# Attention tiles of two heads by 64 queries, with three transposed blocks per two chunks

## The chip, the cores and the metric

The kernel runs on one core of one Trainium2 chip. Its engines are named as in the profile: PE (matmuls; PEld is its weight load), DVE, ACT and POOL (elementwise work), and SP, which issues nearly all transfers. The metric is the device time of one execution in microseconds.

## The reference

One inference step of a two-layer encoder on 1024 prompt frames and 32 sample frames, model width 1024. The first layer is a recurrent mixer, the second a sliding-window attention with 16 query heads and 2 shared key/value heads of width 64. Both are followed by a gated feed-forward network. The change touches the attention only:

```python
CHUNK = 64; WINDOW = 128          # a chunk of 64 queries sees its own and the two chunks before: 192 keys
alibi = -slopes.reshape(N_KV_HEADS, GROUP, 1, 1) * jnp.abs(dist).astype(F32)
bias = jnp.where((key_pos >= 0)[:, None, None, None, :], alibi[None], -jnp.inf)[None]
s = jnp.einsum('bcqhgd,bckhd->bchgqk', q, k).astype(F32) * (HEAD_DIM ** -0.5) + bias
mx = jnp.maximum(jnp.max(s, -1, keepdims=True), sk)      # sk: a learned sink score per head
p = jnp.exp(s - mx)
p = p / (jnp.sum(p, -1, keepdims=True) + jnp.exp(sk - mx))
return jnp.einsum('bchgqk,bckhd->bcqhgd', p.astype(v.dtype), v)
```

The 32 sample queries see 128 cached keys and the 32 keys of the sample.

## The kernel before

**Number format.** Each fp32 operand of a large product is split into a high part (`hi`, cast by ACT) and a remainder (`lo`, subtracted on DVE or POOL). A product is then three matmuls (L402 to L404: hi by hi, hi by lo, lo by hi). In the attention, a query tile carries hi in one half of its partitions and lo in the other, so a product with K's high and low parts is two matmuls.

**Order of the work.** All engines run their instructions in the order in which the program emits them. The order is written out by the program itself: `gemm` emits the dense products and, after every three matmuls, calls `wv.tick(us)` with an estimate of their time. Tasks (Python generators) each count down a pause and then emit their next piece. So attention work is woven between dense matmuls, and a pause is a measure of how much dense work goes in between. `wv.drain` emits a task's pieces at once, with nothing between.

**Tokens.** They come in three groups (`GRP`: 384, 384, 288) for the projections, and in nine blocks of 128 (`CH`; the ninth is the 32 sample tokens). A head pair `j` (0 to 7) is 128 columns of the query projection. `q_group(j, g)` (L1651) projects one pair for one group: 24 matmuls, then ACT writes `qh` (L1657), DVE `ql` (L1658), and `place` sends them with four transfers (L1664, L1665) into a tile `Q` of which there are four. `qh` and `ql` have two buffers each.

**Attention.** `attention` walks over 72 items: head pair `j` by block `b`. Five stages make an item, run in a software pipeline in which `turn` and `values` each lag by one item or more:

- `scores` (L1763, L1764): per head, a product of 128 queries with the 256 keys of this block and the one before (two matmuls of 256 columns, for K's high and low parts); then DVE adds the bias, takes the row minimum (the scores are negated) and writes `s` (L1769). Half of the 256 keys' edge chunks lie outside of a query's window, and the bias holds a large constant there. Block 0 has 128 keys, the sample block 160.
- `soft` (L1781, L1785, L1787): ACT's exponential with its row sum, the reciprocal on DVE, and the scaling on POOL, one per head.
- `turn` (L1807 to L1811): transposes on PE of the 128 by 128 blocks of `s` (two heads by two key blocks, four; two for block 0) into one PSUM tile `T`, which has one buffer; ACT casts it to `hi`, DVE subtracts to `lo`.
- `values` (L1822, L1823): V's 128 keys by 128 columns (high and low part side by side) with `hi` and with `lo`, for both heads at once (256 columns), into the PSUM tile `O` (two buffers).
- `place` (L1831, L1833): ACT copies the lower half of `O`, DVE adds the halves into `act`.

The projections of the pairs to come are emitted in the order `QG`, each once enough items are scored (`ast["scored"]`). Bias tiles `bt`, `sb` are loaded per visit of a head pair, 12 of each (L1689, L1690), with the sinks copied into their last column by POOL (L1697, L1698). `v_turn` (L1736) transposes V through the buffers of `O`, with the casts at L1678 and L1679. One weight half has a place of its own outside of the rotating weight slots (`W.home`, tile `oh`). The weight split is ACT's cast at L237 and POOL's or DVE's subtraction at L239; the load of the next raw weights (`wr`, L163) waits for a raw buffer on SP's queue. After the attention `mixer_out` starts the output projection; `before(0)` (L1900) first drains the attention up to a given item.

## Time and profile before

| | |
|---|---|
| time, median of 3 runs | 2210.78 us (2210.55 to 2211.94) |
| profiled execution: span | 2212.2 us |
| PE busy / DVE / ACT / POOL | 98% / 66% / 46% / 45% |
| granted PE clock, mean | 0.997 |
| matmuls in the whole program | 17086 |
| of these: scores / transposes of s / values | 288 / 272 / 272 |

The span is the time from the first to the last instruction of the one execution that was profiled; there is no other time of that execution, and it stands 1.4 us above the median of the runs. Times are counted from the start of the span. A row of a timeline gives start, duration, engine, line, operation, the tile written and those read, and in brackets the idle time before it and what ended that. "128*128" after a matmul is rows by weight columns of the array. SPq marks the issue of a transfer, not the transfer.

### The profile page before, as it was taken

Reading aid. Unit: us, or ns where it says so; the run is one execution under the profiler, and the core shown is the slowest. Engines: PE = TensorE matmul, PEld = TensorE weight load, DVE = VectorE, ACT = ScalarE, POOL = GpSimd, SP = SyncE. Lnnn points to the kernel's source line nnn. Section 1 sums busy time; section 2 is a strip of 40 time slices with the busy share of each in tenths; the row PEclk is TensorE's granted clock in tenths of the full one; section 3 lists DMA queues with packets and bytes.
Section 4 is the critical chain, followed back from the end, with each engine's and each line's share of the span. In section 5 each row is a group of like instructions: output and inputs, shape, how many; then the busy total and the mean of one; then the engine's idle time right before and its main releaser. Section 6 shows DMA issues by size and latency. Waiting matters only on the chain.

```text
span 2212.2 us, 44257 instructions
## 1 busy us (share of the span) xinstructions
PE 2175.5 (98%) x17086; PEld 2149.4 (97%) x17086; DVE 1455.2 (66%) x2848; ACT 1007.9 (46%) x2259; POOL 989.8 (45%) x982
## 2 busy tenths in 40 slices
PE   9999999999999999999998999999999999999997
PEld 9999999999999999999998999899999999999997
DVE  4465677787656665566667778888666656466657
ACT  4443455464444444321245778756444444432125
POOL 2544210004655555444525776600665555554441
PEclk9999999999999999999999999999999999999999
DMA  5221213212443343797516433511344434397712
GB/s 170 78 62 57 58 40 87 89 39 86 148 156 145 139 147 135 254 329 231 175 57 174 108 100 97 156 63 39 112 161 156 146 127 156 132 344 256 247 56 79
DMA packets 174499, 298.10 MB, mean 135 GB/s; under 512 B 18064, under 2 KB 130760, under 8 KB 174288
## 3 DMA queue, kind: packets, MB, share of 16 engines
q1 hardware_dynamic: 169936, 290.94, 40.0%
q10 hardware_dynamic: 4352, 4.33, 0.6%
q8 instruction: 135, 2.21, 0.4%
q14 instruction: 76, 0.62, 0.1%
HBM read 201.80 MB, written 82.94 MB: 129 GB/s over the span
## 4 chain that ended last, share of the span: by engine, by line
PE 85%; DVE 6%; DMA 3%; ACT 3%; issue 1%; POOL 1%; SPq 0%; ACTq 0%; POOLq 0%; DVEq 0%
PE d L402 10%; PE d L404 10%; PE d L403 10%; PE A L402 9%; PE A L404 9%; PE A L403 9%; PE B L402 7%; PE B L403 7%; PE B L404 7%; DMA sx<-hs_t 1%; PE T L1807 1%; ACT act L505 1%; DMA hs_x<-z 1%; POOL s L1787 1%; PE T L955 1%
## 5 line engine op out<-in xcount | busy, mean ns | idle before, releaser
L239 POOL TENSOR_TENSOR wl_s<-wr,wh_s 128x512 fp32r<-128x512 f32 x224 | 304.1, 1367 | 237.4 <-ACT wh_s L237 168.9
L402 PE MATMUL d<-sx,wh 128*128 128x264 f32 (+2 forms) x1068 | 341.8, 320 | 2.1 <-ACT wh L237 1.8
L239 POOL TENSOR_TENSOR wl_a<-wr,wh_a 128x512 fp32r<-128x512 f32 x112 | 153.5, 1373 | 409.4 <-ACT wh_a L237 288.2
L404 PE MATMUL d<-sx,wl 128*128 128x264 f32 (+2 forms) x1068 | 325.9, 305 | 2.7 <-POOL wl L239 2.7
L403 PE MATMUL d<-sx,wh 128*128 128x264 f32 (+2 forms) x1068 | 325.3, 305 | 0.4 <-DVE sx L433 0.4
L402 PE MATMUL A<-sx,wh_s 128*128 128x264 f32 x896 | 254.7, 284 | 0.0
L403 PE MATMUL A<-sx,wh_s 128*128 128x264 f32 x896 | 254.4, 284 | 0.0
L404 PE MATMUL A<-sx,wl_s 128*128 128x264 f32 x896 | 254.3, 284 | 0.0
L237 ACT CAST wh_s<-wr 128x512 fp32r<-128x512 f32 x224 | 135.7, 618 | 192.6 <-DVE wr L192 102.7
L402 PEld LDWEIGHTS d<-sx,wh 128*128 128x128 f32 x1068 | 202.3, 189 | 5.5 <-ACT wh L237 2.4
L404 PEld LDWEIGHTS d<-sx,wl 128*128 128x128 f32 x1068 | 201.7, 189 | 3.9 <-POOL wl L239 3.6
L403 PEld LDWEIGHTS d<-sx,wh 128*128 128x128 f32 x1068 | 202.6, 190 | 1.5 <-DVE sx L433 0.7
L402 PE MATMUL d<-sx,ex 128*128 128x264 f32 x624 | 180.7, 290 | 0.1
L403 PE MATMUL d<-sx,ex 128*128 128x264 f32 x624 | 177.3, 284 | 0.0
L404 PE MATMUL d<-sx,ex 128*128 128x264 f32 x624 | 177.1, 284 | 0.0
L404 PEld LDWEIGHTS A<-sx,wl_s 128*128 128x128 f32 x896 | 169.0, 189 | 0.0
L402 PEld LDWEIGHTS A<-sx,wh_s 128*128 128x128 f32 x896 | 168.6, 188 | 0.0
L403 PEld LDWEIGHTS A<-sx,wh_s 128*128 128x128 f32 x896 | 168.6, 188 | 0.0
L1323 POOL TENSOR_TENSOR z<-z 128x528 fp32r<-128x528 f32 x76 | 103.2, 1357 | 126.8 <-ACT z L1322 113.3
L239 POOL TENSOR_TENSOR wl<-wr,wh 128x512 fp32r<-128x512 f32 (+2 forms) x81 | 103.9, 1291 | 94.5 <-ACT wh L237 90.7
L1787 POOL TENSOR_SCALAR s<-s,st 128x256 f32<-128x256 f32 (+1 forms) x144 | 122.8, 865 | 46.6 <-DVE st L1785 29.2
L402 PE MATMUL A<-ex,wh_s 128*128 128x264 f32 x448 | 127.5, 285 | 0.0
(352 smaller groups left out, 7247.4 us busy)
## 6 DMA issues: line engine op xcount, KB each, us to landing
wr<-in_gu SPq DMA_DIRECT2D x92, 512.0 KB
hs_x<-z SPq DMA_DIRECT2D x72, 528.0 KB
hs_t<-z SPq DMA_DIRECT2D x64, 528.0 KB
sx<-hs_x SPq DMA_DIRECT2D x112, 264.0 KB
sx<-hs_t SPq DMA_DIRECT2D x64, 264.0 KB
ex<-hs_t SPq DMA_DIRECT2D x64, 264.0 KB
wr<-in_dn SPq DMA_DIRECT2D x32, 512.0 KB
ex<-hs_x SPq DMA_DIRECT2D x32, 264.0 KB
```

Of the source, the lines that this page charges most:

```text
L237: self.nc.scalar.copy(hi, r)
L239: eng.tensor_sub(lo, r, hi.bitcast(F32))
L402: nc.tensor.matmul(out, ah, bh, start=start and k == 0, stop=False, **kw)
L403: nc.tensor.matmul(out, ah, bl, start=False, stop=False, **kw)
L404: nc.tensor.matmul(out, al, bh, start=False, stop=stop and k == last, **kw)
L505: nc.scalar.activation(z, z, AF.Identity, scale=gk, bias=bk)
L955: nc.tensor.matmul(pc[:, : 2 * (DV + 1)], keys, vt[j][:, c], start=True, stop=True)
L1323: eng.tensor_sub(lo.bitcast(F32R), buf(s), hi)
L1787: nc.gpsimd.tensor_scalar_mul(p[:R, h, lo:256], p[:R, h, lo:256], st[:R, 2, h : h + 1])
L1807: nc.tensor.transpose(pt[:nk, i, h, :R], p[:R, h, c : c + nk], ident[:R, :R])
```

## The change

The attention tile becomes two heads by 64 queries (128 rows) with exactly the 192 keys that these see; an item still covers one head pair and one block, now as two such tiles (chunks `c`) side by side in one score bank, so the two banks alternate between items.

- **Q's layout.** `Q` holds, chunk by chunk, 64 tokens of the first head beside 64 of the second; the transfers write pieces of 64 columns, and a group of 288 tokens needs eight. `qh` and `ql` have one buffer.
- **Scores and softmax.** Per chunk two matmuls of 192 columns. The bias has one table of 64 queries by 192 keys per head, on 128 rows, without a constant for unseen keys; the sink column stands before the first chunk and after the second. The scaling on POOL is one product with a broadcast operand for both chunks.
- **Transposes.** The 384 columns of an item's two chunks are three blocks of 128. The middle one holds the last 64 keys of the first chunk and the first 64 of the second.
- **Values.** Two head pairs (items `2 jp` and `2 jp + 1`) share one product per chunk and part. For the middle block V is taken from a tile `VZ` that is zero for the other chunk's keys; `pad_values` fills it by transfers, once for each key/value head.
- **PSUM.** `T` has two buffers and serves V's transposes as well; `O` has one, of a whole bank. `place` runs once per two items.
- **Order.** Head pairs are visited two by two: `JG` lists these twos (`jp`) by group, six items for each entry, and `QG` their projections. The two projections of an entry are emitted one after the other once all items up to the entry before the last are scored. Bias tables are loaded once per `jp`; the place of its own for one weight half goes. `GAP_A` goes from 0.46 to 0.5, and the pause after `values` is 0 and twice that in turn.

The diff, cut to its core:

```diff
-GAP_A = 0.46
+GAP_A = 0.5
...
-        q = Q[j, g] = new(pb, "Q", [P, 2, 384], F32R, bufs=4)
-        h, l = (new(pb, tag, [P, 384], F32R, bufs=2)[:, :n] for tag in ("qh", "ql"))
+        q = Q[j, g] = new(pb, "Q", [P, 2 * 384], F32R, bufs=4)
+        h, l = (new(pb, tag, [P, 384], F32R)[:, :n] for tag in ("qh", "ql"))
...
-                nc.sync.dma_start(q[own, i, :n].bitcast(F32), h[own].bitcast(F32))
-                nc.sync.dma_start(q[other, i, :n].bitcast(F32), l[own].bitcast(F32))
+                for t, src in ((own, h), (other, l)):
+                    for a, m in ((0, LC * (n // LC)), (LC * (n // LC), n % LC)):
+                        if m:
+                            w = min(m, LC)
+                            d = q[t, 2 * a : 2 * a + 2 * m].rearrange("p (c h w) -> p c h w", h=2, w=w)
+                            r = src[own, a : a + m].rearrange("p (c w) -> p c w", w=w)
+                            nc.sync.dma_start(d[:, :, i].bitcast(F32), r.bitcast(F32))
...
+    B, SB = {}, {}
+
+    def load_bias(jp):
+
+        bt = B[jp] = new(pb, "bt", [P, 2, WK + 2], bufs=3)
+        nc.sync.dma_start(bt[:, :, 1 : WK + 1], A["bias"][:, 2 * jp : 2 * jp + 2, :])
+        for h in range(2):
+            r = slice(64 * h, 64 * h + 64)
+            for c in (0, WK + 1):
+                nc.gpsimd.tensor_copy(bt[r, :, c], nsink[r, 4 * jp + h : 4 * jp + 4 : 2])
+
+    def load_sample_bias(jp):
+
+        sb = SB[jp] = new(pb, "sb", [2 * DEC, 2, P + DEC + 1])
+        nc.sync.dma_start(sb[:, :, 1:], A["sbias"][:, 2 * jp : 2 * jp + 2, :])
+        for h in range(2):
+            r = slice(DEC * h, DEC * h + DEC)
+            nc.gpsimd.tensor_copy(sb[r, :, 0], nsink[r, 4 * jp + h : 4 * jp + 4 : 2])
 
     load_bias(0)
-    load_bias(1, False)
+    load_bias(1)
+    load_bias(2)
+    load_sample_bias(0)
...
+    ENDS = (1, 2 * WK + 2)
+    for t in psS:
+        for c in ENDS:
+            nc.vector.memset(t[:, c : c + 1], 0.0)
 
     pb2 = eb.enter_context(pool("pb2"))
-    W.home[U_QB[1][5], 1] = [new(pb2, "oh", [P, D // 2], F32R, bufs=2)[:] for _ in range(2)]
     psb = eb.enter_context(pool("psb", PSUM))
+    VZ = [pb2.tile([P, 8, 2 * HD], F32R, name=f"VZ{i}") for i in range(2)]
+    for i in range(2):
+        nc.gpsimd.memset(VZ[i][64 * (1 - i) : 64 * (2 - i)].bitcast(F32), 0.0)
+
+    def pad_values(tiles, g2):
+
+        for i in range(2):
+            r = slice(64 * i, 64 * i + 64)
+            v = VR[r, tiles, g2].rearrange("p t a d -> p t (a d)")
+            nc.sync.dma_start(VZ[i][r, tiles].bitcast(F32), v.bitcast(F32))
 
...
-                pt = new(psb, "O", [P, 512], bufs=2)
+                pt = new(psb, "T", [P, 512], bufs=2)
                 nc.tensor.transpose(pt[:L, :P], vT[g][:, off : off + L], ident[:])
                 v_parts(c, pt[:L, :P], L)
+                if c % 3 == 2:
+                    pad_values(slice(c - 2, min(c + 1, 8)), 0)
                 ast["v"] = c + 1
...
+    JG = [(0, 0), (1, 0), (0, 1), (0, 2), (1, 1), (1, 2)]
+    JG += [(2, 0), (2, 1), (2, 2), (3, 0), (3, 1), (3, 2)]
+    QG = [(2 * jp + i, g) for jp, g in JG for i in range(2)]
+
+    def last_item(j, g):
+        return 6 * JG.index((j // 2, g)) + 6
+
...
+        def parts(b):
+
+            if b == 0:
+                return [(0, 130, 64, 0, 1 + P), (1, 258, P, 0, 1 + LC)]
+            if b == 8:
+                return [(0, 2, P + DEC, SEQ, 1)]
+            k0 = (b - 1) * P
+            return [(0, 2, WK, k0, 1), (1, 2 + WK, WK, k0 + LC, 1)]
 
         def scores(j, b):
             _, t0, R, g, off = CH[b]
+            jp = j // 2
+            if (j, b) == (4, 0):
+                load_bias(3)
             s = S[j, b] = {}
+            q, g2, ps = Q[j, g], j // 4, psS[j % 2]
+            bias = SB[jp] if b == 8 else B[jp]
+            p = s["p"] = new(pb2, "s", [P, 2 * WK + 4], bufs=4)
             st = s["st"] = new(pb2, "st", [P, 3, 2], bufs=6)
+            n = DEC if b == 8 else LC
+            rows = 2 * n
+            if b == 0:
+                nc.vector.memset(ps[:, 194:195], 0.0)
+            for c, at, nk, k0, _ in parts(b):
+                lhs = q[:, 2 * (off + n * c) : 2 * (off + n * c) + rows]
+                for i, k in enumerate((KH[g2], KL[g2])):
+                    nc.tensor.matmul(ps[:rows, at : at + nk], lhs, k[:, k0 : k0 + nk], start=i == 0, stop=i == 1)
+            for c, at, nk, _, w in parts(b):
+                first = b != 0 and c == 0
+                cols = slice(at - first, at + nk + (not first))
+                bc = slice(w - first, w + nk + (not first))
                 nc.vector.tensor_tensor_reduce(
+                    p[:rows, cols], ps[:rows, cols], bias[:rows, j % 2, bc], 1.0, 3e38,
+                    op0=ALU.add, op1=ALU.min, accum_out=st[:rows, 0, c : c + 1],
                 )
+            if b == 8 and j % 2 and jp < 3:
+                load_sample_bias(jp + 1)
             ast["scored"] += 1
 
         def soft(j, b):
             s = S[j, b]
             p, st = s["p"], s["st"]
+            rows = 2 * DEC if b == 8 else P
+            for c, at, nk, _, _ in parts(b):
+                first = b != 0 and c == 0
+                cols = slice(at - first, at + nk + (not first))
                 nc.scalar.activation(
+                    p[:rows, cols], p[:rows, cols], AF.Exp, bias=st[:rows, 0, c : c + 1], scale=-1.0,
+                    accum_out=st[:rows, 1, c : c + 1],
                 )
+            n = len(parts(b))
+            nc.vector.reciprocal(st[:rows, 2, :n], st[:rows, 1, :n])
+            if 0 < b < 8:
+                w = p[:, 2 : 2 + 2 * WK].rearrange("p (c k) -> p c k", c=2)
+                nc.gpsimd.tensor_mul(w, w, st[:, 2].unsqueeze(2).broadcast_to([P, 2, WK]))
+            else:
+                for c, at, nk, _, _ in parts(b):
+                    w = p[:rows, at : at + nk]
+                    nc.gpsimd.tensor_scalar_mul(w, w, st[:rows, 2, c : c + 1])
+
+        def blocks(b):
 
             if b == 0:
+                return [(1, 130, 64), (2, 258, P)]
             if b == 8:
+                return [(0, 2, P), (1, 130, DEC)]
+            return [(t, 2 + t * P, P) for t in range(3)]
 
         def turn(j, b):
+            s = S.pop((j, b))
             p = s["p"]
+            rows = 2 * DEC if b == 8 else P
+            if j % 2 == 0:
+                pairs_[j // 2, b] = {
+                    tag: new(pb2, tag, [P, 3, 2, P], F32R, bufs=2) for tag in ("hi", "lo")
+                }
+            s = pairs_[j // 2, b]
+            pt = new(psb, "T", [P, 512], bufs=2).rearrange("p (t r) -> p t r", t=4)
+            for t, at, nk in blocks(b):
+                nc.tensor.transpose(pt[:nk, t, :rows], p[:rows, at : at + nk], ident[:rows, :rows])
+            cuts = [(slice(0, 3), P)] if 0 < b < 8 else [(slice(t, t + 1), nk) for t, _, nk in blocks(b)]
+            hi, lo = (s[x][:, :, j % 2, :] for x in ("hi", "lo"))
+            for t, nk in cuts:
+                nc.scalar.copy(hi[:nk, t, :rows], pt[:nk, t, :rows])
+                nc.vector.tensor_sub(lo[:nk, t, :rows], pt[:nk, t, :rows], hi[:nk, t, :rows].bitcast(F32))
 
         def values(j, b):
 
+            if j % 2 == 0:
+                return
+            s = pairs_[j // 2, b]
             g2 = j // 4
+            po = s["po"] = new(psb, "O", [P, 2, 2, P])
+            full = lambda i: VR[:, i, g2].rearrange("p a d -> p (a d)")
+            if b == 0:
+                sums = [[(1, full(0), 64)], [(2, full(0), P)]]
+            elif b == 8:
+                sums = [[(0, full(9), P), (1, full(8), DEC)]]
+            else:
+                sums = [
+                    [(0, full(b - 1), P), (1, VZ[0][:, b], P)],
+                    [(1, VZ[1][:, b - 1], P), (2, full(b), P)],
+                ]
+            rows = 2 * DEC if b == 8 else P
+            for c, terms in enumerate(sums):
+                out = po[:, c, :, :rows]
+                todo = [(v, s[x][:nk, t, :, :rows], nk) for t, v, nk in terms for x in ("hi", "lo")]
+                for i, (v, x, nk) in enumerate(todo):
+                    nc.tensor.matmul(out, v[:nk], x, start=i == 0, stop=i == len(todo) - 1)
+            if (j, b) == (3, 7):
+                pad_values(slice(0, 8), 1)
 
         def place(j, b):
             _, t0, R, g, off = CH[b]
+            ast["placed"] += 1
+            if j % 2 == 0:
+                return
+            po = pairs_.pop((j // 2, b))["po"]
+            n, nc_ = (DEC, 1) if b == 8 else (LC, 2)
+            t = new(pb2, "t", [HD, 2, 2, P])
+            rows = 2 * n
+            nc.scalar.copy(t[:, :nc_, :, :rows], po[HD:, :nc_, :, :rows])
             for h in range(2):
+                out = ACT[h * HD : (h + 1) * HD, j - 1 : j + 1, t0 : t0 + R].rearrange("p j (c q) -> p c j q", c=nc_)
+                a, b_ = (x[:HD, :nc_, :, n * h : n * h + n] for x in (po, t))
+                nc.vector.tensor_add(out, a, b_)
 
         always = lambda j, b: True
         yield 4.0
         yield from pipeline(
+            [(2 * jp + i, 3 * g + b) for jp, g in JG for b in range(3) for i in range(2)],
             [
+                (scores, lambda j, b: ast["ready"] > QG.index((j, CH[b][3])), 0, (gap,) * 8),
                 (soft, always, 0, 0),
+                (turn, always, 1, (gap,) * 8),
+                (values, lambda j, b: ast["v"] > b, 1, (0.0, 2 * gap) * 4),
                 (place, always, 0, 0),
             ],
             (4, 2, 3, 1, 0),
         )
 
 
...
-        while ast["scored"] < 3 * (i - 3):
+        while ast["scored"] < 6 * (i // 2 - 1):
...
-                    lambda k, g: ast["placed"] >= 3 * QG.index((k, g)) + 3,
+                    lambda k, g: ast["placed"] >= last_item(k, g),
...
-            wv.drain(task, lambda: ast["placed"] >= 3 * QG.index((7, 0)) + 3)
+            wv.drain(task, lambda: ast["placed"] >= last_item(7, 0))
```

Of the attention stages the diff shows the lines after the change; those before it are in the listing above. `...` stands for lines left out, the tables of the bias (`_bias`, now 64 queries by 192 keys, and 32 by 160 for the sample) among them.

108 lines of the change are left out of this document (11 added, 97 removed).

## The prediction

> **What bounds the kernel now.** I read the page first: the engines' sums, then the chain that ended last.
>
> ```profile
> span 2212.2 us, 44257 instructions
> ...
> PE 2175.5 (98%) x17086; PEld 2149.4 (97%) x17086; DVE 1455.2 (66%) x2848; ACT 1007.9 (46%) x2259; POOL 989.8 (45%) x982
> ...
> PE 85%; DVE 6%; DMA 3%; ACT 3%; issue 1%; POOL 1%; SPq 0%; ACTq 0%; POOLq 0%; DVEq 0%
> ```
>
> PE is busy nearly throughout and holds 85% of the chain. So the change is worth what it takes off PE's queue, plus the PE idle time that it removes, less what it adds. The busy time by stretches shows where PE idles around the attention, which runs from about 1197 to 1426 us (columns: length, then PE, PEld, DVE, ACT, POOL busy, granted clock, DMA share, GB/s).
>
> ```profile
> 1200.00:1220.00 20.00, 17.34 (x106) 16.12 (x107) 10.40 (x48) 11.18 (x38) 13.75 (x19) 0.91 0.60 159
> ...
> 1260.00:1280.00 20.00, 20.00 (x152) 19.54 (x151) 15.02 (x60) 15.92 (x50) 16.97 (x24) 1.00 0.48 133
> ...
> 1400.00:1420.00 20.00, 17.06 (x130) 15.89 (x129) 15.98 (x53) 14.96 (x46) 17.68 (x19) 0.93 0.39 119
> ```
>
> In the middle PE is full. It idles at the start and at the end of the attention, and there the granted clock dips too (0.91, 0.93). So I cost three things apart: PE's own work, the idle time inside the stage, and the start.
>
> **PE's work, part by part.** Matmuls overlap, so a duration of 280 ns is not a price; the distance between starts is. PE's timeline gives it (start, duration, operation, shape).
>
> ```profile
> 1206.80 0.28 PE L1763 MATMUL psS<-KH,Q 128*128 128x128 f32 x1
> 1206.91 0.28 PE L1764 MATMUL psS<-KL,Q 128*128 128x128 f32 x1
> ...
> 1210.31 0.38 PE L1807 MATMUL T<-ident,s 128*128 128x128 f32 x2
> ...
> 1251.87 0.28 PE L1763 MATMUL psS<-KH,Q 128*128 128x256 f32 x1
> ...
> 1252.34 0.30 PE L402 MATMUL d<-sx,wh 128*128 128x288 f32 x1
> ...
> 1252.75 0.60 PE L1807 MATMUL T<-ident,s 128*128 128x128 f32 x4
> ...
> 1257.66 0.24 PE L1763 MATMUL psS<-KH,Q 128*32 128x160 f32 x1
> ...
> 1257.95 0.38 PE L402 MATMUL d<-sx,wh 128*128 128x384 f32 x1
> ...
> 1414.79 0.19 PE L1822 MATMUL O<-hi,VR 128*128 128x64 f32 x1
> ...
> 1415.36 0.39 PE L402 MATMUL d<-sx,wh 128*128 128x264 f32 x1
> ```
>
> Transposes: a run of four lasts 0.60 us, a run of two 0.38, so one costs (0.60 - 0.38) / 2 = 0.11 us. An inner item (two heads, 128 queries, b = 1 to 7; 56 of them) goes from four to three: 56 x 0.11 = 6.2 us. The eight items of b = 0 keep two. The eight of b = 8 go from four small ones to two: between 0 and 16 x 0.11 = 1.8 us, I take 0.8.
>
> Scores: four products of 256 columns fill 1251.87 to 1252.34, 0.117 us each. They become four of 192 columns, still with 128 weight columns (two heads by 64 queries). No row has that shape. The nearest with 128 weight columns has 128 columns and takes 0.11 (1206.80 to 1206.91), so fewer columns buy almost nothing: 56 x 4 x 0.007 = 1.6 us. The other end is the product of 160 columns with only 32 weight columns: four in 0.29 us, 0.073 each, scaled to 192 columns 0.088: 56 x 4 x 0.029 = 6.5 us. I take 1.6, because the weight width is what the changed shape shares with the first row. The Trainium skill, page "TensorE: Matmul & The Clock Gate", section "Back-to-back issue gap", gives N/2.4 + 2.5 ns, which is an estimate of 82 ns for 192 columns and would make this term 7.8 us; its section "LDWEIGHTS (loading the stationary operand)" gives columns/1.2, 107 ns for 128 weight columns, and the 110 ns above agree with that one. For b = 8, four products of 0.073 become two (weights 32 to 64 columns): 16 x 0.073 = 1.2 us less. For b = 0 there are four at 0.11 in both: nothing.
>
> Values: one product now takes two head pairs, but one 64-query chunk. Per two inner items that is eight products of 256 columns in both kernels: nothing saved. For b = 8, two runs of 0.57 us (1414.79 to 1415.36) become one of four 128-column products, 0.44 to 0.57: four times 0.57 to 0.70, I take 2.5 us.
>
> Sum: 6.2 + 0.8 + 1.6 + 1.2 + 2.5 = **12.3 us less PE work** (10 to 18).
>
> **Idle time inside the stage.** What PE waits for before a run of transposes, and the work that the change makes lighter (rows grouped by line and shape: busy time, mean ns, idle time before it; then two waits from PE's timeline):
>
> ```profile
> L1807 PE MATMUL T<-ident,s 128*128 128x128 f32 x240 | 38.2, 277 | 6.7 <-DVE lo L1811 4.0 <-POOL s L1787 1.1 <-DVE st L1785 1.0
> L1787 POOL TENSOR_SCALAR s<-s,st 128x256 f32<-128x256 f32 x112 | 102.6, 929 | 40.1 <-DVE st L1785 25.1 <-PE psS L1764 7.0 <-PE T L1807 4.2
> L239 POOL TENSOR_TENSOR ex<-wr,ex 128x384 fp32r<-128x384 f32 x24 | 23.5, 1045 | 0.0
> ...
> 1413.60 0.63 PE L1807 MATMUL T<-ident,s 128*128 128x128 f32 x4 [0.95 <-DVE lo L1811]
> ...
> 1417.45 1.09 PE L1807 MATMUL T<-ident,s 128*128 128x128 f32 x4 [1.45 <-DVE lo L1811]
> ```
>
> The waits for lo exist because T has one buffer: a run can't start until DVE has read the last one. T gets two (O drops to one, which is used once per two items). POOL's two products of 0.93 us per inner item become one over 384 columns; the nearest POOL row of two operands and 384 columns is 1.05 us, so the waits for s shrink as well. ACT and DVE read a quarter fewer score and T columns. The 6.7 us of idle time stand for about ten waits; each also loses the overlap of one transpose (0.277 - 0.11 = 0.17 us), 1.7 us, and the dip of the clock after 1417.45 costs (1 - 0.93) x 20 = 1.4 us: 9.8 us in all. What is late next is the exponentials on ACT. I let the change remove **7 us** (3 to 9.8).
>
> **The start.** The head-pair projections write qh and ql (L1657, L1658), which SP's transfers read into Q. The change makes both tiles single-buffered. The chain of waits already runs through this reuse, with two buffers:
>
> ```profile
> 1195.00 5.22 DMA Q<-qh
> 1200.33 0.49 ACT qh L1657
> 1200.82 0.52 ACT wh L237
> 1201.36 0.56 DVE ql L1658
> ...
> 1202.31 0.48 PE O L1736
> ```
>
> Here the fourth projection's qh (1200.33) waited until the second's transfers were out of the buffer; behind it on ACT stands the cast of V, and PE's third transpose of V waits for that. The timelines of ACT, POOL, SP and PE add what sets the third projection's transfers:
>
> ```profile
> 1198.11 0.49 ACT L1657 ACTIVATE qh<-d 128x384 fp32r<-128x384 f32 x1
> ...
> 1199.19 1.27 POOL L239 TENSOR_TENSOR wl<-wr,wh 128x512 fp32r<-128x512 f32 x1 [0.62 <-ACT wh L237]
> ...
> 1200.48 0.33 SPq L163 DMA_DIRECT2D wr<-in_wqb  x1
> 1200.86 0.46 SPq L1664 DMA_DIRECT2D Q<-qh  x1
> ...
> 1202.01 0.60 SPq L1664 DMA_DIRECT2D Q<-qh  x1
> ...
> 1202.31 0.48 PE L1736 MATMUL O<-ident,act 128*128 128x128 f32 x1 [2.80 <-DVE VR L1679]
> ```
>
> With one buffer the third qh waits for the second's transfers, until 1195.00 + 5.22 = 1200.2 instead of 1198.11: 2.1 us. Behind it ACT's weight cast, POOL's rest (L239), SP's load of wr and so the third's transfers move by as much. The fourth qh then waits for the last qh transfer of the third, issued at 1202.01: landing 2.2 us (nothing else in flight, an estimate) to 5.2 us later gives 1204.2 to 1207.2, plus 2.1. Against 1200.33 that is 6 to 9 us, and the V transposes follow it with nothing else in PE's queue to go first. I take **7.5 us more** (5 to 11; the upper end if the smaller pieces also land later).
>
> **Q placed for the last group.** Q is now stored as 64 queries of one head beside 64 of the other, so each transfer is cut into pieces of 64 columns (256 bytes), and a group of 288 tokens takes eight instead of four (288 = 4 x 64 + 32). Transfers for Q go from 96 to 128, those for biases from 24 to 8, and 8 fill the padded values. The projections now come in twos before the next six items. Rows of one 288 group from ACT, POOL and SP, one landing from the chain, and the next projection:
>
> ```profile
> 1256.83 0.42 ACT L1657 ACTIVATE qh<-d 128x288 fp32r<-128x288 f32 x1
> ...
> 1257.83 1.29 POOL L239 TENSOR_TENSOR wl<-wr,wh 128x512 fp32r<-128x512 f32 x1 [0.68 <-ACT wh L237]
> ...
> 1259.15 0.33 SPq L163 DMA_DIRECT2D wr<-in_wqb  x1
> 1259.58 0.46 SPq L1664 DMA_DIRECT2D Q<-qh  x1
> ...
> 1261.37 0.61 SPq L1665 DMA_DIRECT2D Q<-ql  x1
> ...
> 1240.73 4.61 DMA Q<-ql
> ...
> 1263.66 0.49 ACT L1657 ACTIVATE qh<-d 128x384 fp32r<-128x384 f32 x1
> ```
>
> The transfers start 2.75 us after qh, since SP stands at the load of wr until POOL is done, and go out 0.6 us apart. The last reading qh is then the sixth, at 2.75 + 5 x 0.6 = 5.75, free at 8 to 10.4 (landing 2.2 to 4.6). The pair's second projection is ready on PE after 24 products of 288 columns (0.13 each by the 256-column pitch) and two items of 1.3 us, 5.8 us. So ACT, and DVE behind it with ql, stand still for 2 to 4.6 us, four times in the stage (groups of 288, four pairs); exponentials and T copies queue behind. The second Q then lands 7 to 11 us later still, and PE meets its scores after some four items, two of them with no projection between, about 8.7 us. PE loses 0 to 6 us per pair. Between these ends I take 1.25 each, near the lower one, because the items ahead are scored two before their transposes: **5 us more** (0 to 20). Groups of 384 keep four transfers, and 7.5 us pass between two projections: nothing. By the Trainium skill, page "DMA: Bandwidth & Descriptors", section "Specifications", transfers under 512 bytes fall below line rate, while its section "Why small descriptors are slow (HBM only)" exempts SBUF to SBUF, as these are; no row here has such pieces.
>
> **The hand-over.** The last projections' readiness test moves from item 54 to 60 of 72 (L1900), so two operand splits for the first output group come after the last needed item is placed: one ACT cast and one DVE subtraction each, near 0.5 us, **1.5 us** (0 to 3).
>
> ```profile
> L1697 POOL COPY bt<-nsink 128x2 f32<-128x2 f32 x11 | 2.0, 182 | 0.0
> ```
>
> The extra sink columns (12 more such copies before the attention, 2.2 us) and the clearing of the padded values hide in POOL's idle half.
>
> **Sum.** The profiled execution spans 2212.2 us, 1.4 above the median of the runs, 2210.8. -12.3 - 7 + 7.5 + 5 + 1.5 = -5.3, so 2205.5 against the median.
>
> **Rivals.** *The single buffer decides (slower).* Place: qh and ql in the four 288 pairs and at the start. For it: the wait is on the chain already, ACT and DVE are blocked together, and SP's order is fixed. Against it: two items of slack. At 4.5 us per pair (18), 10 at the start, 2 at the hand-over and only 3 us of removed idle time: -12.3 - 3 + 10 + 18 + 2 = +14.7, 2225. It decides once start, pairs and hand-over exceed 12.3 + 7 = 19.3 us. *Gain and loss cancel:* these three come to 18 to 20, 2210. *Cheaper scores, no new waits:* the score product follows its columns (4.9 more), the start loses 5 to 6, the pairs nothing: -12.3 - 4.9 - 7 + 6 = -18, 2192.5. Beside it, the gap rule of the Trainium skill named above, taken alone, would make it 2199. *The change does less than its words:* the values products keep their number; that is in the sum.
>
> **How the numbers follow.** This kernel's measurement can tell 0.2%, 4.4 us. Forecast 2205.5 (2200 to 2210): 0.42, of which three quarters lie beyond 4.4 us; cancelling: 0.15; slower rival: 0.30; cheap scores: 0.13. Faster: 0.32 + 0.13 = 0.45; same: 0.10 + 0.15 = 0.25; slower: 0.30. The range, 2193 to 2223, goes to the middle of both outer rivals and leaves out about 2 in 10. The forecast's own is 2200 to 2210.
>
> **What would show it.** Right: three transposes per inner item at 0.11, score starts 0.11 apart, hardly a wait of T for lo; a PE gap of about 10 us before the third transpose of V instead of 2.8, released from qh by a transfer. Wrong: score starts 0.08 apart; no longer gap at the start; or PE waits of 3 us and more for Q, four times, after the 288 groups.

## The result, and the profile after

The changed kernel takes 2246.73 us (median, 2245.01 to 2250.07) against 2210.86 for the kernel before: 1.0162 times as long, with a 95% interval of 1.0147 to 1.0176. The forecast was 2205.5 with a range of 2193 to 2223, so the time lies 36 us above the kernel before and 24 above the range. (A ratio sets a kernel against the kernel before, run beside it. The kernel before took 2210.9 to 2212.7 on these occasions, so where a difference of medians and a ratio seem to differ, the ratio counts.)

The page of the changed kernel, in the same lines as before:

```profile
span 2243.3 us, 43908 instructions
...
PE 2181.9 (97%) x16982; PEld 2150.6 (96%) x16982; DVE 1428.2 (64%) x2778; ACT 989.4 (44%) x2215; POOL 933.0 (42%) x920
...
PE 85%; DVE 5%; ACT 3%; DMA 3%; issue 1%; POOL 1%; SPq 1%; ACTq 0%; POOLq 0%; DVEq 0%
```

PE has 104 matmuls less and each other engine less busy time, and still the span is 31 us longer. The dense products are the same 14736 in both kernels (768 more, all in the first 270 us, are left out), so the start of the k-th can be set against the start of the k-th (us). Between 7848 and 8207 some projections of 288 and of 384 tokens have changed places; at 7872 this makes the difference about 1 us too large, at 8160 about 1 us too small, and at the other rows nothing:

```
dense product    before     after   difference
         7488    1153.8    1154.7        0.9
         7728    1195.9    1197.0        1.1
         7776    1215.4    1227.2       11.8    (third V transpose lies between)
         7872    1242.3    1257.3       15.0
         7920    1256.1    1277.4       21.3    (first group of 288)
         8016    1284.7    1313.8       29.1    (second)
         8160    1334.0    1366.9       32.9    (third)
         8352    1393.4    1429.2       35.8    (fourth)
         8496    1428.9    1460.3       31.4    (attention over)
        14400    2152.3    2183.4       31.1
```

Before product 7728 and after 8496 nothing moves. Within, the loss comes in steps, and the stretches of the changed kernel show what they look like (columns as in the prediction's table):

```profile
1200.00:1220.00 20.00, 8.72 (x35) 7.76 (x34) 3.75 (x21) 5.25 (x16) 9.50 (x10) 0.70 0.62 151
1220.00:1240.00 20.00, 17.35 (x112) 16.32 (x110) 9.68 (x48) 10.21 (x41) 6.60 (x9) 0.87 0.03 7
1260.00:1280.00 20.00, 14.60 (x95) 14.04 (x93) 8.56 (x36) 10.86 (x34) 9.14 (x9) 0.83 0.37 97
1300.00:1320.00 20.00, 15.87 (x106) 15.20 (x106) 10.71 (x47) 13.35 (x44) 10.70 (x11) 0.91 0.32 83
1360.00:1380.00 20.00, 16.50 (x103) 16.17 (x104) 11.80 (x50) 13.21 (x42) 8.23 (x9) 0.83 0.25 64
```

The stretch 1260 to 1280, where PE was busy for all of the 20 us, has 14.6 now, and every other engine is emptier too: no engine took over as the bound, all of them stood still together. The sums of the waits in the attention (1180 to 1460; us in total, times, longest) say for what:

```profile
ACT qh L1659 <- DMA Q<-qh: 23.8, 8, 6.5
...
DVE ql L1660 <- ACT qh L1659: 12.2, 5, 7.0
...
PE T L1854 <- POOL s L1829: 15.7, 7, 5.3
...
PE T L1756 <- DVE VR L1686: 9.7, 1, 9.7
...
PE psS L1801 <- DVE psS L1797: 7.3, 8, 1.3
```

Before, ACT's qh waited 0.7 us in all for a transfer of Q. Now it waits 23.8, and PE's three long kinds of wait (15.7 + 9.7 + 7.3 = 32.7 us) are new or larger. One of the blocks, in the timeline (the second projection of a pair on the first group of 288):

```profile
1263.01 0.41 ACT L1659 ACTIVATE qh<-d 128x288 fp32r<-128x288 f32 x1 [1.90 <-DMA Q<-qh]
...
1265.77 1.25 SPq L1672 DMA_DIRECT2D Q<-qh  x2
1265.79 0.49 PE L1854 MATMUL T<-ident,s 128*128 128x128 f32 x3
...
1269.72 1.25 SPq L1672 DMA_DIRECT2D Q<-ql  x2
1270.97 0.41 ACT L1659 ACTIVATE qh<-d 128x288 fp32r<-128x288 f32 x1 [4.17 <-DMA Q<-qh]
...
1271.79 0.46 ACT L1821 ACTIVATE s<-s,st 128x193 f32<-128x193 f32 x1
...
1272.80 0.17 DVE L1826 RECIPROCAL st<-st 128x2 f32<-128x2 f32 x1
...
1273.19 0.83 POOL L1829 TENSOR_TENSOR s<-s,st 128x384 f32<-128x384 f32 x1
...
1274.07 0.90 PE L1854 MATMUL T<-ident,s 128*128 128x128 f32 x3 [5.30 <-POOL s L1829]
```

The first group's qh is written at 1263.0. Its eight transfers go out from 1265.77 to 1270.97, one every 0.65 us. The second group's qh needs the same buffer and holds ACT until 1270.97; the exponentials stand behind it on ACT, then come the reciprocal, the multiplication and PE's transposes, whose 5.3 us of waiting name POOL although the cause is a transfer three engines back.

The other new wait is short and comes eight times:

```profile
1231.00 0.84 DVE L1900 TENSOR_TENSOR act<-O,t 64x256 f32<-64x256 f32 x2
...
1231.87 0.56 DVE L1859 TENSOR_TENSOR lo<-T,hi 128x384 fp32r<-128x384 f32 x1
...
1232.46 0.17 DVE L1826 RECIPROCAL st<-st 128x2 f32<-128x2 f32 x1
1232.64 0.06 DVE L1797 MEMSET psS<- 128x1 f32 x1
1232.75 0.30 PE L1801 MATMUL psS<-KH,Q 128*128 128x64 f32 x1 [1.32 <-DVE psS L1797]
```

For a tile of b = 0 the change clears one score column just ahead of the products. The clearing takes 0.06 us, but it stands on DVE's queue behind the placing, a subtraction and a reciprocal that needs ACT's sums, 1.6 us of work in these rows, and PE, which in the kernel before went straight on, now waits for DVE's queue.

Over the stretch from dense product 7728 to 8496, PE's time divides into distances between starts of up to 0.4 us (work, dense or attention's own) and longer ones (idle time). The ledger for the kernels that follow, each from its one profiled execution (us). Such an execution lies up to 3.6 us off its kernel's median, so differences of 2 or 3 us between two rows aren't safe:

```
kernel                              stretch   dense   attention   over 0.4 us (times)
before                               232.9    123.1      91.3       18.5 (19)
after                                263.3    126.5      88.4       48.4 (28)
e1  two qh and ql                    235.6    122.9      83.4       29.3 (28)
e2  no memset                        254.5    125.0      84.9       44.6 (22)
e3  both                             228.0    124.5      79.7       23.8 (22)
e4  before, one qh and ql            244.9    122.8      91.6       30.5 (22)
e5  after, spread                    249.5    122.7      81.8       45.1 (29)
e7  e3, one T and two O              235.8    123.8      80.7       31.3 (32)
e8  e3, spread                       226.7    123.3      79.9       23.5 (23)
e9  before, two T and one O          255.0    120.7      93.9       40.4 (45)
e11 e8, scores later                 225.3    123.5      79.6       22.2 (24)
e13 e3, five Q                       228.2    124.7      82.2       21.3 (19)
e14 e11, pause 0.58                  225.9    123.2      81.0       21.7 (20)
e15 e11, pause 0.44                  225.3    122.3      80.7       22.3 (22)
e16 e11, transposes a tile later     231.9    122.9      81.6       27.4 (31)
e17 before, transposes a tile later  231.7    123.9      90.9       17.0 (17)
e19 e3, even pauses                  223.1    122.1      79.2       21.8 (24)
e18 e11, even pauses                 221.1    122.3      79.0       19.8 (19)
```

### The profile page after: what moved, and what is told of

It reads as the page before. It is cut to its first block, busy times and chain, and to the rows that moved or that the text cites. A ratio compares the mean times of both kernels' runs of the same rounds, so it can differ in the third digit from the quotient of the medians.

```text
span 2243.3 us, 43908 instructions
## 1 busy us (share of the span) xinstructions
PE 2181.9 (97%) x16982; PEld 2150.6 (96%) x16982; DVE 1428.2 (64%) x2778; ACT 989.4 (44%) x2215; POOL 933.0 (42%) x920
## 4 chain that ended last, share of the span: by engine, by line
PE 85%; DVE 5%; ACT 3%; DMA 3%; issue 1%; POOL 1%; SPq 1%; ACTq 0%; POOLq 0%; DVEq 0%
PE d L404 10%; PE d L406 10%; PE d L405 10%; PE A L404 9%; PE A L406 9%; PE A L405 9%; PE B L404 7%; PE B L405 7%; PE B L406 7%; PE O L1883 1%; PE psS L1801 1%; PE T L1854 1%; ACT act L507 1%; POOL wl L241 1%; DMA hs_x<-z 1%
## 5 line engine op out<-in xcount | busy, mean ns | idle before, releaser
L404 PE MATMUL d<-sx,wh 128*128 128x264 f32 (+2 forms) x1080 | 349.4, 324 | 1.4 <-ACT wh L239 1.3
L406 PE MATMUL d<-sx,wl 128*128 128x264 f32 (+2 forms) x1080 | 331.5, 307 | 2.1 <-POOL wl L241 2.1
L405 PE MATMUL d<-sx,wh 128*128 128x264 f32 (+2 forms) x1080 | 331.6, 307 | 0.2 <-DVE sx L435 0.2
L404 PEld LDWEIGHTS d<-sx,wh 128*128 128x128 f32 x1080 | 206.8, 192 | 5.8 <-ACT wh L239 2.5
L405 PEld LDWEIGHTS d<-sx,wh 128*128 128x128 f32 x1080 | 206.9, 192 | 1.8 <-DVE sx L435 0.8
L404 PE MATMUL A<-ex,wh_s 128*128 128x264 f32 x448 | 127.5, 285 | 0.0
L405 PE MATMUL A<-ex,wh_s 128*128 128x264 f32 x448 | 127.1, 284 | 0.0
```

What stands on the lines that cost most here:

```text
L404: nc.tensor.matmul(out, ah, bh, start=start and k == 0, stop=False, **kw)
L405: nc.tensor.matmul(out, ah, bl, start=False, stop=False, **kw)
L406: nc.tensor.matmul(out, al, bh, start=False, stop=stop and k == last, **kw)
```

## The experiments

Theory A: the single qh and ql hold ACT and DVE, and through them everything. Theory B: the transfers of Q are late in themselves. Theory C: the clearing of the score column.

**The second buffer back.**

```diff
-        h, l = (new(pb, tag, [P, 384], F32R)[:, :n] for tag in ("qh", "ql"))
+        h, l = (new(pb, tag, [P, 384], F32R, bufs=2)[:, :n] for tag in ("qh", "ql"))
```

> The changed kernel with two buffers for qh and ql, as the kernel before has them; nothing else differs. Theory A (the single buffer: ACT and DVE, standing at qh and ql until the transfers of the group before have read them, stop exp and so POOL's multiplication and the transposes): the gap ahead of the third V transpose falls from 10.0 to about 2.8 us, and the gaps of 5.6, 4.0 and 5.0 us ahead of the transposes go; 7 + 19 = 26 us less, 2246.7 - 26 = about 2221 us. Theory B (the Q transfers themselves are late, eight of 0.62 us to issue per group of 288): only the start comes back, 2239 us, and the score products wait for Q in place of the transposes waiting for s. Theory C (DVE's memset of one score column ahead of every b = 0 tile is the main loss): 2240 us or more.

2218.85 us, ratio to before 1.0032 (1.0019 to 1.0045): 27.9 us less than the changed kernel. Theory A. The 9.7 us ahead of the third V transpose are gone, and the transposes' waits are half, none of them longer than 1.5 us (1180 to 1460):

```profile
PE T L1854 <- POOL s L1829: 7.6, 7, 1.5
PE psS L1801 <- DVE psS L1797: 7.4, 8, 1.3
...
PE psS L1801 <- DMA Q<-ql: 1.5, 2, 1.1
```

**No clearing in the loop.** The short window of b = 0 goes to score columns of its own, with a sink column cleared once.

```diff
-    ENDS = (1, 2 * WK + 2)
+    ENDS = (1, 2 * WK + 2, 454)
...
-            if b == 0:
-                nc.vector.memset(ps[:, 194:195], 0.0)
+            def pcol(c, at):
+                return 390 if b == 0 and c == 0 else at
```

> The changed kernel with the short window of b = 0 put at score columns 390 to 453, whose sink column is cleared once at the start, so that no memset stands ahead of the score products; single qh and ql as in the changed kernel. Theory C: the eight waits of PE for DVE's psS (7.3 to 9.7 us in sum) go, and the time falls by 8 to 10 us, to about 2238 us. Theory A: the waits go, but part of them turns into a longer wait for qh behind them; 2 to 6 us less, 2241 to 2245 us.

2236.54 us, ratio 1.0113 (1.0098 to 1.0128), 10.2 us less: theory C is right on its size, as a second cause beside A. In this profile the first block is 2.5 us longer than in the changed kernel's (12.2 in place of 9.7), and the waits behind qh stay. So only 3.8 of the 8.8 us that the ledger saves are idle time; the other 5.0 are PE's work, which the section on the prediction puts down to the clock:

```profile
ACT qh L1659 <- DMA Q<-qh: 31.0, 10, 6.9
...
PE T L1857 <- POOL s L1832: 16.6, 8, 5.3
...
PE T L1756 <- DVE VR L1686: 12.2, 1, 12.2
```

**Both.**

> Two buffers for qh and ql and no memset in the loop, together. Theory A and C add up: 2246.7 - 26 - 9 = about 2212 us, as long as the kernel before. If the terms of the prediction for PE's work (-12.3) and for the idle time inside the stage (-7) hold once the waits are gone, 2190 to 2200 us. Theory B: 2230 us.

2209.75 us, ratio 0.9989 (0.9979 to 0.9998): the two add up (27.9 + 10.2 = 38.1; 37.0 measured; by the ratios 28.7 + 10.8 and 38.2), and the kernel is back where the kernel before is. The 2190 to 2200 that the prediction's gains would give do not come. PE's waits there (1195 to 1430):

```profile
PE T L1857 <- POOL s L1832: 7.5, 7, 1.5
PE psS L1803 <- DMA Q<-ql: 3.4, 3, 1.2
```

**The kernel before with one qh and ql.**

```diff
-        h, l = (new(pb, tag, [P, 384], F32R, bufs=2)[:, :n] for tag in ("qh", "ql"))
+        h, l = (new(pb, tag, [P, 384], F32R)[:, :n] for tag in ("qh", "ql"))
```

> The kernel before with one buffer each for qh and ql, the only edit. Theory A: the loss at the start appears here too (about 7 us), and of the groups of 288, which come one at a time with four transfers each, little: 0 to 4 us; 2218 to 2222 us. Theory B: the single buffer is not the cause, 2211 to 2213 us.

2228.41 us, ratio 1.0072 (1.0057 to 1.0087): 16 us more, the cause shown alone in the old kernel, and more than either theory expected. The start (columns as in the timelines above):

```profile
1209.45 0.49 ACT L1657 ACTIVATE qh<-d 128x384 fp32r<-128x384 f32 x1 [6.72 <-DMA Q<-qh]
...
1210.99 0.48 PE L1736 MATMUL O<-ident,act 128*128 128x128 f32 x1 [10.52 <-DVE VR L1679]
...
1360.73 0.41 ACT L1657 ACTIVATE qh<-d 128x288 fp32r<-128x288 f32 x1 [2.93 <-DMA Q<-qh]
...
1363.52 0.41 PE L1807 MATMUL T<-ident,s 128*128 128x128 f32 x2 [3.70 <-DVE lo L1811]
```

10.5 us at the start in place of 2.8, and one block of 3.7 at a group of 288; the other groups, one at a time, pass. Of the ledger's 12.0 us more, all are idle time.

**The two projections of a pair apart**, with single buffers.

```diff
-        while ast["scored"] < 6 * (i // 2 - 1):
+        while ast["scored"] < 6 * (i // 2 - 1) + 3 * (i % 2):
```

> The changed kernel, single buffers, but the second projection of a pair is held back until three more tiles are scored, so that the two no longer stand back to back. Theory A with its place (the second group's qh waits for the eight transfers of the first, just issued): the gaps of 5.6, 4.0 and 5.0 us ahead of the transposes shrink to under 2 us each, the gap of 10 us at the start stays; 10 to 18 us less, 2229 to 2237 us. Rival (one buffer blocks wherever the groups stand, since eight transfers take about 5 us to issue after each group): 2243 to 2248 us.

2233.05 us, ratio 1.0099 (1.0082 to 1.0116), 13.7 less. The blocks at the groups of 288 come from two projections back to back on one buffer; the longest wait of PE for POOL's s falls from 5.3 to 2.5 us, the 11.6 us at the start stay, and score products now wait for Q 7.5 us in seven waits. So what the change does badly is the single buffer and its own new order together.

**The same edit on top of the two cures.**

> Two buffers for qh and ql, no memset in the loop, and the second projection of a pair held back by three tiles. If what is left of the idle time with two buffers comes from the two projections standing together (score products wait 3.4 us for Q, transposes wait 17 us for POOL behind two weight splits of 1.26 us): 3 to 8 us less than 2209.75, 2202 to 2207 us. Rival (POOL and ACT are late whatever the order): 2208 to 2212 us.

2211.34 us, ratio 0.9996 (0.9987 to 1.0005): no gain over 0.9989. The waits for Q grew, it seems because the second group is now projected closer to its use:

```profile
PE psS L1803 <- DMA Q<-ql: 7.8, 6, 1.9
PE T L1857 <- POOL s L1832: 3.2, 5, 1.3
```

**The buffers of T and O, from both sides.** First the kernel before with the change's two T and one O, then the cured kernel with the old one T and two O.

```diff
-                pt = new(psb, "O", [P, 512], bufs=2)
+                pt = new(psb, "T", [P, 512], bufs=2)
...
-            pt = new(psb, "T", [P, 2, 2, P])
+            pt = new(psb, "T", [P, 512], bufs=2).rearrange("p (i h r) -> p i h r", i=2, h=2)
...
-            po = s["po"] = new(psb, "O", [P, 2, P], bufs=2)
+            po = s["po"] = new(psb, "O", [P, 2, P])
```

> The kernel before with two buffers for T and one for O (the V transposes moved to T with them), the only edits. By the prediction's term for idle time, the waits of the transposes for lo (4.0 us on the profile before) and part of the waits for the multiplication behind them go: 3 to 7 us less, 2205 to 2209 us. Rival (the waits move to the next in line: POOL's multiplication ahead of the transposes, and the values products now wait for the one O): 2211 to 2216 us.

2238.00 us, ratio 1.0118 (1.0103 to 1.0133): 26 us slower, outside of both expectations. No wait for lo is left, but with one O and values products in every item PE waits for the placing:

```profile
PE O L1822 <- DVE act L1833: 16.4, 26, 1.4
```

> Two buffers for qh and ql and no memset in the loop, with one buffer for T and two for O, as the kernel before has them. By the prediction's term for idle time this gives back 3 to 7 us: 2213 to 2217 us against 2209.75. Rival (the buffers of T are not what the transposes wait for): 2207 to 2211 us.

2217.36 us, ratio 1.0023 (1.0013 to 1.0033): 7.6 more than the cured kernel. In the new tile the second T, less what the single O costs, is worth what the prediction said. PE waits for the one O 0.7 us in all in the cured kernel, where O is used once per two items. But the waits for lo that the second T takes away are 11.2 us in the new tile, not the 4.0 of the kernel before:

```profile
PE T L1857 <- DVE lo L1862: 11.2, 14, 2.4
PE T L1857 <- DVE st L1829: 5.3, 5, 2.1
```

**What is left: Q's lateness.** One run writes the score products into PE's queue later (on top of the two cures and the spread), one gives Q a fifth buffer and starts the first projection of a pair earlier.

```diff
     def q_made():
-        yield 4.0
+        yield 7.0
```

> As the kernel with two buffers, no memset and the second projection held back, but a group's score products are written into PE's queue 7.0 instead of 4.0 planned us after its projection, so that weight products stand there while the transfers land. If PE's waits for Q (7.8 us in six waits in that kernel's profile) are time lost: they go, 4 to 8 us less, 2203 to 2207 us. Rival (scores then run late and the transposes wait for POOL in their place): 2208 to 2213 us.

2206.47 us, ratio 0.9975 (0.9965 to 0.9986): at the near edge of the expected gain. PE's waits for Q fell from 7.8 to 4.0 us, those for POOL are 4.3 + 3.5.

```diff
-        q = Q[j, g] = new(pb, "Q", [P, 2 * 384], F32R, bufs=4)
+        q = Q[j, g] = new(pb, "Q", [P, 2 * 384], F32R, bufs=5)
...
-        while ast["scored"] < 6 * (i // 2 - 1):
+        while ast["scored"] < 6 * (i // 2 - 1) - 3 * (1 - i % 2):
```

> Two buffers for qh and ql, no memset in the loop, five buffers for Q in place of four (paid for by two buffers for bt instead of three, its third load moved into the loop, and seven value tiles instead of eight in each half-empty copy), and the first projection of each pair three tiles earlier, so that the two stand three tiles apart and each is done six tiles ahead of its use. If the waits for Q and the two projections standing together are what is left: no wait of PE for Q over 0.5 us, and 5 to 10 us less than 2209.75, 2200 to 2205 us. Rival (POOL's multiplication, behind the weight splits in POOL's queue, decides whatever the order): 2207 to 2212 us.

2208.23 us, ratio 0.9978 (0.9969 to 0.9988), the rival's time. No wait for Q is left on PE; the transposes' wait for POOL is as long as before:

```profile
PE T L1857 <- POOL s L1832: 7.8, 7, 1.8
```

**The pause of attention's steps**, on e11: 0.58 and 0.44 in place of 0.50.

```diff
-GAP_A = 0.5
+GAP_A = 0.58
```

> The kernel with all four edits of before (two buffers for qh and ql, no memset, second projection held back, scores 7.0 planned us after the projection), with the pause between steps of attention at 0.58 planned us in place of the change's 0.50. If the transposes wait for POOL since steps stand too close for the chain exp, reciprocal, multiplication: their waits (4.3 us on PE) go, 3 to 6 us less than 2206.5, 2200 to 2204 us. Rival (weight products run out ahead of the end and attention's tail stands alone): 2207 to 2215 us.

> The same with the pause at 0.44. If steps stand too close already: 2209 to 2215 us. Rival (the pause does not matter, since the chip's own waits set the steps): within 2 us of 2206.5.

2206.67 us (0.9974, 0.9964 to 0.9984) and 2210.22 (0.9994, 0.9984 to 1.0004). More room gives nothing, against the 3 to 6 us expected, and less costs some 4 us, as expected; the profiled execution with 0.44 was not one of the longer ones, so where these 4 us lie isn't shown.

**The transposes one tile later**, on e11 and on the kernel before.

```diff
-                (turn, always, 1, (gap,) * 8),
+                (turn, always, 2, (gap,) * 8),
```

> The kernel with all four edits and the pause of 0.50, with the transposes of a tile written into PE's queue one tile later (two tiles of softmax ahead of them instead of one). If what is left of the idle time is the length of the chain from score products through exp, reciprocal and POOL's multiplication to the transposes: PE's waits for POOL's s (some 12 us of gaps ahead of transposes) go, and the time falls by 6 to 12 us, 2194 to 2200 us: the terms of the prediction for PE's work and idle time would then be there. Rival (the next in line, O's one buffer or the score products, waits in its place): 2203 to 2209 us.

> The kernel before with its transposes one tile later, the only edit. Here the transposes wait for lo in the one T (4.0 us) more than for POOL (1.1 us): 2210 to 2214 us. If the chain is as late here: 3 to 6 us less.

2214.71 us and 2213.47, both 1.0006 (0.9997 to 1.0016). On the kernel before that is no change, as expected. On e11 the waits for POOL's s on PE fell from 4.3 to 0.4 us, as expected of a late chain, and yet the time rose by 7 to 8 us, past the rival's 2209 too. The values products, which wait for the one O, V's transposes and the score products wait in its place:

```profile
PE O L1886 <- DVE act L1903: 3.8, 5, 1.2
PE T L1756 <- DVE VR L1686: 2.6, 2, 1.5
...
PE psS L1803 <- DMA Q<-ql: 2.3, 2, 2.1
PE O L1886 <- ACT sx L434: 1.8, 1, 1.8
PE psS L1803 <- DVE st L1809: 1.8, 3, 0.8
...
PE T L1857 <- POOL s L1832: 0.4, 1, 0.4
```

**Even pauses.** The change has no pause after an even head pair's tile, which has no values products, and two after an odd one's.

```diff
-                (values, lambda j, b: ast["v"] > b, 1, (0.0, 2 * gap) * 4),
+                (values, lambda j, b: ast["v"] > b, 1, (gap,) * 8),
```

> Two buffers for qh and ql and no memset in the loop, with one pause of 0.50 after each tile's values step in place of the change's none after the even head pair and two after the odd one. In the profile without this edit first transposes of successive tiles start 3.44 and 1.88 us apart in turn (medians), in the kernel before 2.91 and 2.87. If this uneven pace is why the transposes wait for POOL's multiplication (1.88 us is too short for the chain behind one tile): the gaps ahead of transposes shrink by about half (some 13 us of them now), 4 to 8 us less than 2209.75, 2202 to 2206 us. Rival (the waits only move): 2208 to 2213 us.

> The same even pauses with all four edits (two buffers, no memset, second projection held back, scores 7.0 planned us after the projection), 2206.5 us with uneven pauses. If the uneven pace is the cause of what is left: 2199 to 2203 us. Rival: 2205 to 2210 us.

2206.30 us (0.9975, 0.9965 to 0.9986) and 2204.99 (0.9969, 0.9960 to 0.9979). By the ratios that is 0.14% below e3 and 0.06% below e11, their partners with uneven pauses, with overlapping intervals: the direction is the expected one, but a gain isn't shown, and both miss their ranges. First transposes are 2.98 and 2.37 us apart in e19, and PE's waits for POOL's products are 7.7 us in place of e3's 9.6, not half. The last kernel has the lowest median of all, 0.31% below the kernel before, with an interval that overlaps those of e11, e13, e14 and e19.

## Why the prediction was wrong

The signs that the prediction had named for being right came, and the time was still 41 us above the forecast. Three steps failed: the slack that it credited to PE behind the groups of 288, the clearing that it put at nothing, and the idle time inside the stage, which rose.

**PE's work: -12.3 us. Right.** In the ledger attention's own work falls from 91.3 us before to 79.0 in the last kernel, 12.3 less, and to 79.7 in e3; over all cured kernels it is 9.1 to 12.3 less, so the equal tenth is luck. In the changed kernel itself it is only 2.9 less, for a reason that comes below. By parts, in the last kernel: transposes 24.4 to 17.3 (7.1, predicted 7.0), scores 32.7 to 28.8 (3.9, predicted 2.8), values 33.8 to 32.4 (1.4, predicted 2.5). The score products of 192 columns start 0.111 us apart (median), so the row with the same weight width was the right one, and the rival of cheaper scores falls. By the gap rule of the Trainium skill (page "TensorE: Matmul & The Clock Gate", section "Back-to-back issue gap") they would stand 82 ns apart, but the page gives that rule for an isolated matmul and says that for small widths it counts too little, since it leaves out the weight load; the measured 0.111 is near the 107 ns of its section "LDWEIGHTS (loading the stationary operand)".

**The start: +7.5. Right.** The predicted gap of about 10 us stands ahead of the third V transpose, 9.7 us in place of 2.8, released through qh by a transfer:

```profile
1208.76 0.49 ACT L1659 ACTIVATE qh<-d 128x384 fp32r<-128x384 f32 x1 [6.54 <-DMA Q<-qh]
...
1210.50 0.47 PE L1756 MATMUL T<-ident,act 128*128 128x128 f32 x1 [9.67 <-DVE VR L1686]
```

By the dense products the stage is 10.7 us later behind it than in the kernel before (11.8 - 1.1), near the upper end of 5 to 11, and 12.6 later than in e1. The gap itself is 6.9 longer; two waits for the clearing (1.6 us) and slower matmuls lie in the same step. The old kernel with one buffer has the gap too, 10.5.

**The 288 groups: +5 (0 to 20). The mechanism was right and the size wrong.** Against e1, at the same rows of the table of dense products, the changed kernel loses 12.6 us at the start and then 5.5, 3.8, 3.8 and 2.1 at the four pairs: 15 us, three times what I took and within the 0 to 20. The step that failed is the slack. I expected ACT to stand for 2 to 4.6 us per pair (4.17 in the row above) and then took 1.25 for PE, since the items ahead are scored two before their transposes. That slack isn't there: the exponentials of those items stand on ACT behind the same qh. PE waited 5.3 us for s in the block shown, more than ACT did. The sign of being wrong that the prediction named, waits of PE for Q itself, did not come (1.1 us in all): PE stood at the transposes, behind the engines that qh held, before it came to those scores.

**The slower clock, priced once (1.4 us) and not where the change adds gaps.** After gaps of this length the next matmuls run at about half speed: three transposes took 0.49 us at 1265.79 and 0.90 at 1274.07, behind the gap of 5.3 us. The granted clock is 0.70 to 0.91 in the stretches with blocks, and 0.50 around the end of this gap (first line, of the changed kernel). With the blocks cured it is full in the stretches of the first three groups of 288 (the other lines, of e3):

```profile
1272.90:1279.70 6.80, 5.63 (x23) 5.46 (x24) 4.69 (x21) 4.68 (x14) 4.01 (x5) 0.50 0.41 111
...
1260.00:1280.00 20.00, 20.00 (x151) 19.15 (x149) 12.39 (x49) 11.22 (x37) 6.40 (x10) 1.00 0.24 55
1300.00:1320.00 20.00, 20.00 (x138) 18.58 (x137) 13.07 (x59) 13.09 (x48) 7.26 (x16) 1.00 0.36 87
1360.00:1380.00 20.00, 18.81 (x140) 17.75 (x138) 14.21 (x59) 15.31 (x52) 8.99 (x11) 1.00 0.53 133
```

In the ledger attention's own work is 88.4 us in the changed kernel and 79.7 in e3, with the same products: 8.7 us, and 2 on the dense ones, an estimate of what the clock adds to the idle time. It is part of the prices of the start, the pairs and the clearing, not one more beside them. The sum of the idle time does not set it: e5 idles nearly as long as the changed kernel (45.1 us), with shorter blocks at the groups of 288, and its attention's own work is 81.8. The Trainium skill (the same page, section "HAM oscillation — how this bites in real kernels") gives as a rule that PE shall have no idle gap over some 3.4 us. The blocks, 3.7 to 9.7 us each, agree with it, but the clock also dips to 0.93 in the kernel before from 1400 to 1420, where the longest wait is 1.45 us: the length of one gap isn't the whole rule here.

**The wait for the clearing: missed, 10.2 us.** The prediction priced the POOL instructions that the change adds and passed over one column cleared by DVE ahead of the b = 0 scores, so it put this at nothing without a reason. The row to ask for was DVE's queue at that place: the placing of two head pairs (0.84 us), a subtraction and a reciprocal that needs ACT's sums.

**The idle time inside the stage: -7. Wrong in sign.** Idle time went from 18.5 us to 23.8 in e3, 5.3 more, though the blocks and the clearing are cured there. The second T does give 7.6 (e7), but against the waits of the new tile (11.2 us for lo), not of the old (4.0). What adds to the idle time and would have had to be in the sum: waits for Q (0.4 us before; 3.4 in e3, where two groups stand together, 7.8 in e8, where they don't; gone in e13), and waits for POOL's s (1.1 us before, 7.5 in e3), with successive transposes 3.44 and 1.88 us apart in turn (e3) in place of 2.91 and 2.87 before. That the uneven pace is the cause isn't shown. With even pauses and later scores the idle time is 19.8 us, 1.3 above the kernel before, and no run of the new tile brought it below. Each wait that was taken away alone let another take its place (e8, e13, e16). Why the last 20 us stay, isn't settled: several engines' queues share them, and on top of the two cures no single edit took off more than some 5 us.

**The hand-over: +1.5. Not seen.** From dense product 8352 to 8496 the kernel before takes 35.5 us, the changed one 31.1, e3 31.6: what the later readiness test may cost is less than what the lighter tiles save there.

**The sum.** 27.9 for the single buffer and 10.2 for the clearing, less 2.6 (e3 against before), come to the 36 measured (35.5). Against the forecast the pairs cost 10 us more than their term, the start 3 to 5, the clearing 10 and the idle time 12 (5.3 in place of -7): 35 to 37 of the 41 us; the rest isn't placed. The rival "the single buffer decides" named the place and the price per pair (4.5 against 3.8) nearly right, and at 2225 still fell 22 us short, by the clearing (10) and by the idle time (5.3 more in place of 3 less). The base was read a little wrong too: in all runs after it an execution takes 1.7 to 2.1 us more than its span, so the profiled execution before, with its span of 2212.2, took about 2214 (an estimate), some 3 us above the median instead of 1.4.

## What to carry to other kernels

A buffer that a transfer has to read holds more than its writer: ask what stands behind the writer on its engine, follow that chain to the bound, and give the tile ahead no credit for slack if its own next step is in the same queue. A one-column clearing on another engine costs what that engine's queue is late, not its 0.06 us, so put it where it is done once. And a gain in work on the busiest engine can be forecast rightly and still not show, until the order and the pace of the steps around it are made anew.

## What was not expected of the hardware

The smaller pieces of Q were not seen to be slow. Their transfers (pieces of 256 bytes, 128 for the last 32 tokens) land 2.9 us after their issue in the median (1.8 to 5.0), as the view of the tile Q in the changed kernel has it for the 16 of 128 whose landing it knows:

```profile
DMA to landing us min/median/max: 1.8/2.9/5.0
```

For the kernel before the view gives no landing; the two on its chain, quoted in the prediction, took 4.61 and 5.22 us, too few for a comparison of like with like. What the layout costs for certain is the number of transfers, about 0.65 us of SP's queue for each in the block shown. This doesn't contradict the exemption that the prediction cited from the Trainium skill, page "DMA: Bandwidth & Descriptors", section "Why small descriptors are slow (HBM only)".
